# More buffers for two small operands, and a later back transpose, in the gated-DeltaNet part of a hybrid encoder layer

## The chip, the cores and the metric

The kernel runs on one core of one Trainium2 chip. The metric is the device time of one execution in microseconds (us); the number given for a kernel is the median of several runs. The engines of the core are named as in the profile: PE (TensorE, matrix products and transposes; PEld is its weight load), DVE (VectorE), ACT (ScalarE), POOL (GpSimd) and SP (SyncE, which here only issues DMAs; its queue is written SPq).

## The reference: what is computed

One encoder layer over x of 2048 rows by 1024 columns. One combined projection of the normalised x is split into the inputs of three mixing branches and a gate z; the three outputs are joined, multiplied by silu(z), projected back and added to x:

```python
h = rms_norm(x, norm_pre_w[l])
proj = h @ w_in[l]
aq, ak, av, bqkv, ba, bb, mq, z = jnp.split(proj, pts, axis=-1)
# A: softmax attention, 8 query heads, 2 key heads, rotary positions
y_a = axial_gqa_attention(aq, ak, av)
# B: gated DeltaNet, 4 heads of width 128, both directions, chunks of 64
bqkv = centred_short_conv(bqkv, conv_w[l])          # 5 taps, then silu
bq, bk, bv = (t.reshape(b, s, B_HEADS, HEAD_DIM) for t in jnp.split(bqkv, 3, axis=-1))
y_b = bidir_gated_deltanet(bq, bk, bv, ba, bb, a_log[l], dt_bias[l])
#   g = -exp(a_log) * softplus(ba + dt_bias);  beta = sigmoid(bb)
#   q and k are divided by their norms; g is summed up inside a chunk;
#   per chunk: k k^T and q k^T times exp(g_i - g_j), a triangular solve,
#   then a scan over the chunks
# M: cross-attention of 4 heads into 256 memory rows
y_m = memory_cross_attention(mq, mk, mv)
mix = jnp.concatenate([y_a, y_b, y_m], axis=-1) * jax.nn.silu(z)
x = x + rms_norm(mix @ w_out[l], norm_post_w[l])
```

Everything that the change touches belongs to branch B.

## The kernel before, in words

The program is one function. Its loops emit instructions in the written order; a planner then simulates a timeline with its own durations and from it fixes, once and for all, the order of the instructions of each engine. Stretches where `pin(...)` is on keep their written order on the engines named. Each engine works through its list in order; where engines depend on each other they wait on semaphores. All operations go through a small wrapper, so the profile shows line L51 for nearly everything, and L77 for the DMAs that POOL issues; the names of the tiles tell them apart. A tile's `bufs` is the number of rooms that its successive uses take in turn.

The stages, with the times at which they stand in the profiled execution:

- 0 to 328 us: loads, normalisation of x, and the projections of branches A and M.
- **Stage s2** (L584 to L694), 328 to about 631 us: the q, k and v of branch B. There are 48 slots: 12 groups of 128 channels (`ch` 0 to 3 are q, 4 to 7 are k, 8 to 11 are v) by 4 blocks of 512 rows (`b`). Each slot goes through four steps at different lags. `b_proj` (lag 0) makes 24 matmuls into the PSUM tile `b` and copies it to `xb` on ACT. `b_conv` (lag 2) is the five-tap convolution, five DVE instructions into `y`, a tanh on ACT (`th`) and one DVE instruction into `sv`. `b_turn` (lag 5) transposes `sv` on PE, into `bs` for q and into `bt` for k and v. For q, ACT squares and sums it. For v, ACT copies it to `kt`, which goes to DRAM (`bx`). For k, ACT squares it, DVE reduces it (`kss`) and runs a short chain of 128x4 instructions for the inverse root (`rs_x`, `rs_u`, `kr`), DVE multiplies into `kt`, and `kt` goes to `bx`. `b_back` (lag 7, k only) transposes `kt` back on PE into `bu`; ACT copies that to `ku`, which goes to `bx` too. The same slots also carry small side work: `wor` (loads and squares of w_out, an ACT instruction behind a DMA each) and `v` (a split of branch A's values).
- `fill(48)` (L816) emits the first steps of the z projection; after it PE is pinned to the written order (L817). `fill(n)` always means n more matmuls, with what belongs to them, of the z and mq projections. Per 24 matmuls of z: `zt` (tanh on ACT), `zg` (DVE) and a `gate` DMA on POOL's queue; every second group of channels also has new weights `wraw` and `wparts`, made by POOL, ACT and DVE.
- **The gate part of stage s3** (L820 to L906): 72 fill matmuls; then, in pool `s3g`, softplus and sigmoid of the per-row gates: a chain of 128x128 DVE instructions over `xa`, `ax`, `u`, `s_`, `s` and `acc` with exponentials on ACT, which ends in `gg` and `beta`. `psg` is the product of `gg` with a triangle on PE, 40 fill matmuls follow, then transposes `gr` into the table `grow`, which stage s3a reads.
- **Stage s3a** (L909 to L932), about 650 to 755 us: 32 turns (two head pairs by 16 chunks of 128 rows, pool `s3r`). A turn loads `kq` (the chunk's back-transposed k, and q) from `bx`, multiplies it on PE (`pg`), makes the decay exponents on PE (`pe`), exponentials on ACT (`dd`), five DVE products into `nit`, a DMA of `nit` to `NI`, and 10 fill matmuls.
- Then, on DVE, the triangular inverse of all chunks of a head pair (L935 to L961): `ni` is loaded from `NI` by 16 small DMAs, and pairs of `tm`/`rr` instructions follow. The `ni` loads of head pair 0 stand in SP's queue among the turns of head pair 1.
- From about 850 us: the scan of branch B, the attention of A and M, and the output projection.

The lines that the change touches stand in `b_turn` (L635), in the slot loop (L687 and L692) and in the s3a loop (L914):

```python
kt = p.tile([128, 4, 128], F32, tag="kt", name=f"kt{ch}_{b}", bufs=2)          # L635
for n in range(len(slots) + 7):                                                # L687
    for lag, f in ((0, b_proj), (2, b_conv), (5, b_turn), (7, b_back)):        # L692
kq = p.tile([128, 2, 2, 128], F32, tag="kq", name=f"kq{nm}", bufs=3)           # L914
```

Of the kernel before, what the change touches and what calls it, by code (L numbers as in the profile page):

```python
# [11 lines left out]
F32 = mybir.dt.float32  # L12
# [25 lines left out]
def hybrid_layer(ctx: ExitStack, tc: tile.TileContext, t: dict, out, dbg=None):  # L38
# [238 lines left out]
    def load_group(*args, **kw):  # L277
        _, loaded = begin_group(*args, **kw)
        return loaded
# [177 lines left out]
    with tc.tile_pool(name="s1", bufs=1) as p:  # L457
# [49 lines left out]
        for which in range(2):  # L507
# [20 lines left out]
            for g in range(1 if which == 0 else 4):  # L528
                wg, (qcs,) = nxt
                for b in range(4):  # L530
# [4 lines left out]
                    nm = f"{which}_{g}_{b}"  # L535
# [48 lines left out]
    with tc.tile_pool(name="s2", bufs=1) as p:  # L584
        wg, bcs, xbs, svs, kts_ = {0: nxt[0]}, {0: nxt[1]}, {}, {}, {}

        def b_proj(ch, b):
            g, u = ch // 2, ch % 2
            if u == 1 and b == 0:
                if g < 5:  # L590
                    wg[g + 1], bcs[g + 1] = load_group([(1536 + 256 * (g + 1), 256)])
                else:
                    _, wg[6] = z_load(4)
            if b == 0:
                xb = xbs[ch] = p.tile([128, S + 4], F32, tag="xb", name=f"xb{ch}", bufs=2)
                V.memset(xb[:, 0:2], 0.0)
                V.memset(xb[:, S + 2:S + 4], 0.0)
            ps = mm_ps(f"b{ch}_{b}")
            n = 0
            for kc in range(KC):  # L600
                hi, lo = wg[g][kc // 4]
                sl = slice(u * 128, u * 128 + 128)
                for wt, ht in ((hi, 0), (hi, 1), (lo, 0)):
                    T.matmul(ps, wt[:, kc % 4, sl], hT[b][ht][:, kc, :], start=(n == 0), stop=(n == 3 * KC - 1))
                    n += 1
            A.activation(xbs[ch][:, 2 + 512 * b:2 + 512 * (b + 1)], ps, AF.Copy, scale=bcs[g][0])

        def b_conv(ch, b):
            xb, o = xbs[ch], 512 * b
            y = p.tile([128, 512], F32, tag="y", name=f"y{ch}_{b}", bufs=2)  # L610
            V.tensor_scalar(y, xb[:, o:o + 512], convw[:, ch, 0:1], None, op0=ALU.mult)
            for k in range(1, 5):
                V.scalar_tensor_tensor(y, xb[:, o + k:o + k + 512], convw[:, ch, k:k + 1], y, op0=ALU.mult, op1=ALU.add)
            th = p.tile([128, 512], F32, tag="th", name=f"th{ch}_{b}", bufs=2)
            A.activation(th, y, AF.Tanh)
            sv = svs[ch, b] = p.tile([128, 4, 128], F32, tag="sv", name=f"sv{ch}_{b}", bufs=2)
            V.scalar_tensor_tensor(sv.rearrange("p a b -> p (a b)"), th, 1.0, y, op0=ALU.add, op1=ALU.mult)

        def b_turn(ch, b):
            kind, hd = ch // 4, ch % 4  # L620
            hp, hh = hd // 2, hd % 2
            sv = svs.pop((ch, b))
            if kind == 0:
                dma(bx(hp, b, 1, hh), sv)
                pt = tp_ps(f"bs{ch}_{b}", (128, 4, 128))
                sq = p.tile([128, 4, 128], F32, tag="sq", name=f"sq{ch}_{b}")
                for j in range(4):
                    T.transpose(pt[:, j, :], sv[:, j, :], ident)
                for j in range(4):
                    A.activation(sq[:, j, :], pt[:, j, :], AF.Square, accum_out=ssq[:, hd, 4 * b + j:4 * b + j + 1])  # L630
                return
            pt = tp_ps(f"bt{ch}_{b}", (128, 4, 128))
            for j in range(4):
                T.transpose(pt[:, j, :], sv[:, j, :], ident)
            kt = p.tile([128, 4, 128], F32, tag="kt", name=f"kt{ch}_{b}", bufs=2)  # L635
            if kind == 2:
                A.copy(kt, pt)
                dma(bx(hp, b, 3, hh), kt)
                return
            sq = p.tile([128, 4, 128], F32, tag="sq", name=f"sq{ch}_{b}")  # L640
            A.activation(sq, pt, AF.Square)
            ks = p.tile([128, 4], F32, tag="kss", name=f"kss{ch}_{b}", bufs=2)
            V.tensor_reduce(ks, sq, axis=AX.X, op=ALU.add)
            kr = p.tile([128, 4], F32, tag="kr", name=f"kr{ch}_{b}", bufs=2)
            rsqrt(p, kr, ks, [128, 4], 1.0, EPS)
            V.tensor_tensor(kt, pt, kr.unsqueeze(2).to_broadcast([128, 4, 128]), op=ALU.mult)
            dma(bx(hp, b, 2, hh), kt)
            kts_[ch, b] = kt

        def b_back(ch, b):  # L650
            if (ch, b) not in kts_:
                return
            kt = kts_.pop((ch, b))
            hp, hh = (ch % 4) // 2, ch % 2
            pt = tp_ps(f"bu{ch}_{b}", (128, 4, 128))
            for j in range(4):
                T.transpose(pt[:, j, :], kt[:, j, :], ident)
            ku = p.tile([128, 4, 128], F32, tag="ku", name=f"ku{ch}_{b}")
            A.copy(ku, pt)
            dma(bx(hp, b, 0, hh), ku)  # L660

        def wo_sums(kc):

            raw = p.tile([128, D], F32, tag="wor", name=f"wor{kc}")
            dma(raw, t["w_out"][0, kc * 128:(kc + 1) * 128, :])
            A.activation(raw, raw, AF.Square, accum_out=wosq[:, kc // 2, kc % 2:kc % 2 + 1])

        v32s, v16s = {}, {}

        def v_split(tb, k):  # L670

            if k == 0:
                v32s[tb] = p.tile([128, 256], F32, tag="v32", name=f"v32_{tb}")
                dma(v32s[tb], v_d[tb])
                v16s[tb] = p.tile([128, 2, 256], F16, tag="v16", name=f"v16_{tb}")
                return
            pin(A, V)
            if k == 1:
                A.activation(v16s[tb][:, 0], v32s[tb], AF.Copy, scale=vs)
            else:  # L680
                v = v16s.pop(tb)
                V.scalar_tensor_tensor(v[:, 1], v32s.pop(tb), vs, v[:, 0], op0=ALU.mult, op1=ALU.subtract)
                dma(v16_d[:, :, tb, :], v)
            pin()

        slots = [(ch, b) for ch in range(12) for b in range(4)]
        for n in range(len(slots) + 7):  # L687
            if n < 3 * TB:
                v_split(n // 3, n % 3)
                if n % 3 == 1:  # L690
                    wo_sums(n // 3)
            for lag, f in ((0, b_proj), (2, b_conv), (5, b_turn), (7, b_back)):  # L692
                if 0 <= n - lag < len(slots):
                    f(*slots[n - lag])  # L694
    first_z = wg[6]
# [213 lines left out]
    with tc.tile_pool(name="s3a", bufs=1) as sv0:  # L909
        p = rows  # L910
        for hp in range(2):
            for c in range(TB):
                nm = f"{hp}_{c}"
                kq = p.tile([128, 2, 2, 128], F32, tag="kq", name=f"kq{nm}", bufs=3)  # L914
                dma(kq, bx_d[hp, c, :, 0:2])
                pg = tp_ps(f"pg{nm}", (128, 2, 2, 128))
                for h in range(2):
                    T.matmul(pg[:, :, h, :], kq[:, 0, h, :], kq[:, :, h, :], start=True, stop=True)
                pe = tp_ps(f"pe{nm}", (128, 2, 2, 128))
                T.matmul(pe, pick[:, c:c + 1].to_broadcast([96, 128]), grow[:, :, 2 * hp:2 * hp + 2, :], start=True, stop=False)  # L920
                T.matmul(pe, identb, maskb, start=False, stop=True)
                dd = p.tile([128, 2, 2, 128], F32, tag="dd", name=f"dd{nm}", bufs=2)
                for d in range(2):
                    for h in range(2):
                        A.activation(dd[:, d, h, :], pe[:, d, h, :], AF.Exp, bias=ngc[:, d, 2 * hp + h, c:c + 1])
                ni = p.tile([128, 2, 2, 2, 128], F32, tag="nit", name=f"nit{nm}", bufs=2)
                V.tensor_tensor(ni[:, :, 1], dd, pg[:, 1].unsqueeze(1).to_broadcast([128, 2, 2, 128]), op=ALU.mult)
                for d in range(2):
                    for h in range(2):
                        V.scalar_tensor_tensor(ni[:, d, 0, h, :], pg[:, 0, h, :], beta[:, d, 2 * hp + h, c:c + 1], dd[:, d, h, :], op0=ALU.mult, op1=ALU.mult)  # L930
                dma(NI_d[hp, :, c].rearrange("d p n h i -> p d (n h i)"), ni.rearrange("p d n h i -> p d (n h i)"))
                fill(FILL[1])  # L932
        pr_pool.close()
        sv1 = pr_pool.enter_context(tc.tile_pool(name="s3c", bufs=1, side="right"))
        for hp in range(2):  # L935
            p = (sv0, sv1)[hp]
# [226 lines left out]
    p = p5.enter_context(tc.tile_pool(name="at", bufs=1))  # L1163
    kt, vt, PT = at["k"], at["v"], at["PT"]
# [267 lines left out]
    for i in range(len(blocks) + LAG + 1):  # L1432
# [27 lines left out]
        for tb in range(2):  # L1460
            n = i - len(blocks) - 2 * tb - LAG + 4
# [43 lines left out]
    with ExitStack() as es:  # L1505
        p = es.enter_context(tc.tile_pool(name="op", bufs=1))
# [101 lines left out]
```

## Time and profile before

| what | us |
|---|---|
| median of 3 runs | 2408.82 (2407.42 to 2410.19) |
| the profiled execution | 2418.02 |
| its span, first to last instruction | 2416.0 |
| PE busy | 2316.7 (96%) |
| DVE busy | 1637.6 (68%) |
| ACT busy | 1298.9 (54%) |
| POOL busy | 703.2 (29%) |
| mean granted clock of PE | 0.989 |

Rows of a timeline give the start in us, the duration, the engine, line, operation, "out<-in" with its shapes, the number of instructions in the row (xN) and, in brackets, the idle time of the engine just before it with the instruction or DMA whose end released it. A row of windows gives a stretch of the span, its length, and the busy time and number of instructions of PE, PEld, DVE, ACT and POOL; then the clock granted to PE (1.00 is full), the share of the DMA engines that was busy and the rate in GB/s. A row of groups gives the instructions of one kind, their count, their busy time in us and the mean in ns, and the idle time ahead of them.

### The profile page before, as it was taken

Reading aid. Unit: us, or ns where it says so; the run is one execution under the profiler, and the core shown is the slowest. Engines: PE = TensorE matmul, PEld = TensorE weight load, DVE = VectorE, ACT = ScalarE, POOL = GpSimd, SP = SyncE. Lnnn points to the kernel's source line nnn. Section 1 sums busy time; section 2 is a strip of 40 time slices with the busy share of each in tenths; the row PEclk is TensorE's granted clock in tenths of the full one; section 3 lists DMA queues with packets and bytes.
Section 4 is the critical chain, followed back from the end, with each engine's and each line's share of the span. In section 5 each row is a group of like instructions: output and inputs, shape, how many; then the busy total and the mean of one; then the engine's idle time right before and its main releaser. Section 6 shows DMA issues by size and latency. Waiting matters only on the chain. (4 is left out here: it accounts for less than half of the span.)

```text
span 2416.0 us, 42155 instructions
## 1 busy us (share of the span) xinstructions
PE 2316.7 (96%) x15838; PEld 1466.6 (61%) x15846; DVE 1637.6 (68%) x3304; ACT 1298.9 (54%) x2508; POOL 703.2 (29%) x432
## 2 busy tenths in 40 slices
PE   6999999999999899999999999999999999899998
PEld 6888864455554347667664566666666666544443
DVE  6687658999758745555553778777888877355553
ACT  5634436544443145555543888888888788111110
POOL 0155431112211221121020554444444445122120
PEclk9999999999999999999999999999999999999999
DMA  6457656334487466677865999999999999775551
GB/s 232 144 137 162 123 118 188 101 111 126 146 254 214 106 201 212 205 221 219 249 201 192 232 248 242 246 240 244 239 250 241 246 240 231 202 248 187 178 183 53
DMA packets 949500, 471.58 MB, mean 195 GB/s; under 512 B 723184, under 2 KB 898864, under 8 KB 949040
## 3 DMA queue, kind: packets, MB, share of 16 engines
q1 hardware_dynamic: 936848, 425.89, 69.6%
q0 software_dynamic: 12448, 43.00, 5.3%
q8 instruction: 125, 2.05, 0.3%
q14 instruction: 79, 0.65, 0.1%
HBM read 207.60 MB, written 108.10 MB: 131 GB/s over the span
## 5 line engine op out<-in xcount | busy, mean ns | idle before, releaser
L51 PEld LDWEIGHTS <-wparts 128*128 128x128 f16 x3072 | 294.9, 99 | 324.2 <-issue 18.1
L51 POOL TENSOR_TENSOR hla<-Pa,hla 128x1281 f16<-128x1281 f32 x128 | 335.8, 2624 | 343.1 <-DVE hla L51 320.2
L51 DVE TENSOR_REDUCE mxa<-sa 128x1 f32<-128x1024 f32 x256 | 313.1, 1223 | 132.3 <-PE sa L51 132.2
L51 PE MATMUL sa<-K,qa 128*128 128x512 f16 x1536 | 373.8, 379 | 21.2 <-ACT Pa L51 10.0
L51 PE MATMUL z<-hT,wparts 128*128 128x512 f16 x1536 | 378.4, 384 | 4.1 <-POOL wparts L51 2.9
L51 PE MATMUL pva<-PT,V 128*128 128x256 f16 x3072 | 376.4, 273 | 0.0
L51 ACT ACTIVATE Pa<-sa,mxa,misc 128x1024 f32<-128x1024 f32 x256 | 305.9, 1199 | 97.8 <-POOL hla L51 81.0
L51 PEld LDWEIGHTS <-V 128*128 128x128 f16 x3072 | 300.6, 98 | 84.9
L51 PE MATMUL o<-wo,mhl 128*128 128x512 f16 x1416 | 309.5, 382 | 6.3 <-ACT mhl L51 3.8
L51 PE MATMUL b<-hT,wparts 128*128 128x512 f16 x1152 | 258.1, 381 | 0.0
L51 PEld LDWEIGHTS <-mhl 128*128 128x128 f16 x1464 | 143.7, 98 | 181.9 <-DVE mhl L51 4.2
L51 PEld LDWEIGHTS <-qa 128*128 128x128 f16 x1536 | 150.1, 98 | 157.0 <-issue 27.0
L51 ACT CAST hla<-Pa 128x2048 f16<-128x2048 f32 x128 | 243.0, 1899 | 4.2
L51 PEld LDWEIGHTS <-hT 128*128 128x128 f16 x2304 | 224.8, 98 | 30.4 <-DVE we L51 1.7
L51 PE MATMUL q<-wparts,hT 128*128 128x256 f16 x1920 | 210.3, 273 | 1.4 <-DVE we L51 1.4
L77 POOL DMA_DIRECT2D gate<-zg x64 | 35.4, 554 | 423.7 <-DVE zg L51 288.1
L51 POOL TENSOR_SCALAR wraw<-wraw,wsc 128x1024 f32<-128x1024 f32 x21 | 69.1, 3292 | 288.4 <-DVE wy L51 197.5
L51 ACT CAST mhl<-mr 128x2048 f16<-128x2048 f32 (+1 forms) x16 | 29.1, 1818 | 221.7 <-PE o L51 172.8
L51 DVE SCALAR_TENSOR_TENSOR y<-xb,convw,y 128x512 f32<-128x512 f32 x192 | 145.8, 771 | 2.0
L51 POOL TENSOR_TENSOR mg<-mg 128x1536 f32<-128x1536 f32 (+1 forms) x16 | 59.4, 3712 | 234.1 <-DMA mg<-r 171.2
L51 DVE SCALAR_TENSOR_TENSOR hla<-Pa,hla 128x768 f16<-128x768 f32 x128 | 121.6, 950 | 0.0
L51 DVE TENSOR_TENSOR mhl<-mr,mhl 128x2048 f16<-128x2048 f32 (+1 forms) x16 | 45.2, 2824 | 89.3 <-ACT mhl L51 89.3
(354 smaller groups left out, 3165.4 us busy)
## 6 DMA issues: line engine op xcount, KB each, us to landing
xx<-bx SPq DMA_DIRECT2D x64, 512.0 KB, 6.0
wraw<-in_w_in POOLq DMA_DIRECT2D x42, 512.0 KB, 5.3
wor<-in_w_out SPq DMA_DIRECT2D x32, 512.0 KB, 4.3
gate<-zg POOLq DMA_DIRECT2D x64, 256.0 KB, 4.0
NI<-nit SPq DMA_DIRECT2D x32, 512.0 KB, 3.0
mr<-mix SPq DMA_DIRECT2D x13, 1024.0 KB, 6.1
mg<-r SPq DMA_DIRECT2D x13, 768.0 KB
x<-in_x SPq DMA_DIRECT2D x16, 512.0 KB, 6.3
```

The costliest lines, as they stand in the source:

```text
L51: ins = f(*args, **kw)
L77: nc.gpsimd.dma_start(to, of)
```

## The change

Three constants are changed; no operation is added or removed.

```diff
@@ -632,7 +632,7 @@
             pt = tp_ps(f"bt{ch}_{b}", (128, 4, 128))
             for j in range(4):
                 T.transpose(pt[:, j, :], sv[:, j, :], ident)
-            kt = p.tile([128, 4, 128], F32, tag="kt", name=f"kt{ch}_{b}", bufs=2)
+            kt = p.tile([128, 4, 128], F32, tag="kt", name=f"kt{ch}_{b}", bufs=3)
             if kind == 2:
                 A.copy(kt, pt)
                 dma(bx(hp, b, 3, hh), kt)
@@ -684,12 +684,12 @@
             pin()
 
         slots = [(ch, b) for ch in range(12) for b in range(4)]
-        for n in range(len(slots) + 7):
+        for n in range(len(slots) + 8):
             if n < 3 * TB:
                 v_split(n // 3, n % 3)
                 if n % 3 == 1:
                     wo_sums(n // 3)
-            for lag, f in ((0, b_proj), (2, b_conv), (5, b_turn), (7, b_back)):
+            for lag, f in ((0, b_proj), (2, b_conv), (5, b_turn), (8, b_back)):
                 if 0 <= n - lag < len(slots):
                     f(*slots[n - lag])
     first_z = wg[6]
@@ -911,7 +911,7 @@
         for hp in range(2):
             for c in range(TB):
                 nm = f"{hp}_{c}"
-                kq = p.tile([128, 2, 2, 128], F32, tag="kq", name=f"kq{nm}", bufs=3)
+                kq = p.tile([128, 2, 2, 128], F32, tag="kq", name=f"kq{nm}", bufs=5)
                 dma(kq, bx_d[hp, c, :, 0:2])
                 pg = tp_ps(f"pg{nm}", (128, 2, 2, 128))
                 for h in range(2):
```

A `kt` room is 2,048 bytes per partition, a `kq` room also. The pool s2 grows up from the left of the memory; the pools s3r (with `kq`) and s3g (with the softplus tiles, behind s3r) grow down from the right. In the built program before, s2 ends at byte 188,032 of a partition and s3g begins at 192,160. In the changed one s2 ends at 190,080 (one `kt` room more) and s3g begins at 188,064 (two `kq` rooms lower). So there 2,016 bytes belong to both: `xa`, `ax`, `u` and `s_` of the softplus lie over bytes of s2, and the planner lets the first of them wait until s2 is released, which the last `kt` and its DMA do.

The order of the instructions changes on every engine between the q slots of s2 and the gate part of s3, and on SP also in s3a; before and after that it is the same. Three places are shown.

The first is DVE's list at the end of s2, where the last two `sv` of the v channels (s2's last work on DVE) are followed by what comes next. Before:

```order
L51 SCALAR_TENSOR_TENSOR sv_2_7028<-th_2_7026,y_2_7020 128x512
L51 SCALAR_TENSOR_TENSOR sv_3_7046<-th_3_7044,y_3_7038 128x512
L51 TENSOR_TENSOR gg<-acc,nal 128x64 x2
L51 TENSOR_TENSOR beta<-u,s__7294 128x128
L51 TENSOR_SCALAR rs_x<-ssq 128x64
L51 TENSOR_SCALAR qs<-rs_x 128x64
L51 SCALAR_TENSOR_TENSOR zg_0_7115<-zt_0_7113,z_0_7088 128x512
```

In the changed kernel the place begins so (`qs`, `rs_x` and `rs_u` are the inverse norms of q, which both kernels compute here):

```order
L51 SCALAR_TENSOR_TENSOR sv_3_7046<-th_3_7044,y_3_7038 128x512
L51 TENSOR_TENSOR xa<-ab,dtb 128x64 x2
L51 TENSOR_SCALAR rs_x<-ssq 128x64
L51 TENSOR_SCALAR ax<-xa 128x128
L51 TENSOR_SCALAR qs<-rs_x 128x64
L51 TENSOR_TENSOR ax<-ax,xa 128x128
L51 SCALAR_TENSOR_TENSOR zg_0_7115<-zt_0_7113,z_0_7088 128x512
L51 SCALAR_TENSOR_TENSOR rs_u<-qs 128x64
L51 SCALAR_TENSOR_TENSOR zg_1_7159<-zt_1_7157,z_1_7132 128x512
```

and 42 rows further on it reads:

```order
L51 TENSOR_SCALAR acc<-acc 128x128
L51 SCALAR_TENSOR_TENSOR zg_0_7265<-zt_0_7263,z_0_7238 128x512
L51 TENSOR_TENSOR acc<-acc,s__7294 128x128
L51 SCALAR_TENSOR_TENSOR acc<-xa,acc 128x128
L51 TENSOR_TENSOR gg<-acc,nal 128x64 x2
L51 COPY xa<-ab 128x64 x2
L51 TENSOR_SCALAR ax<-xa 128x128
```

So the whole softplus, which stood among the q slots (`xa` between the convolutions some 550 rows earlier), now stands behind the last `sv`, and `gg` behind it, where `gg` was the first instruction; the five `zg`, the `qs` chain and one `wparts` stand ahead of `gg` instead of behind it. `psg` has the same place on PE in both.

The second place is ACT's list among the q slots. Before:

```order
L51 ACTIVATE xb_4325<-b_1_4366,wc_3744 128x512
L51 ACTIVATE wor_4464,wosq<-wor_4464 128x1024
L51 ACTIVATE sq_0_4404,ssq<-bs_0_4403 128x128 x4
L51 ACTIVATE wor_4617,wosq<-wor_4617 128x1024
L51 ACTIVATE xb_4325<-b_2_4416,wc_3744 128x512
L51 ACTIVATE th_2_4360<-y_2_4354 128x512
```

Now:

```order
L51 ACTIVATE xb_4325<-b_1_4366,wc_3744 128x512
L51 ACTIVATE wor_4464,wosq<-wor_4464 128x1024
L51 ACTIVATE sq_0_4404,ssq<-bs_0_4403 128x128 x4
L51 ACTIVATE th_2_4360<-y_2_4354 128x512
L51 ACTIVATE th_3_4398<-y_3_4392 128x512
L51 ACTIVATE xb_4325<-b_2_4416,wc_3744 128x512
```

The tanh of this slot has moved ahead of a `wor`, which needs a load of w_out.

The third place is SP's queue where s3a goes from head pair 0 to head pair 1 (`kq_3` to `kq_8` and `nit_0` on are of pair 1, `nit_14` and `nit_15` of pair 0, `ni` are the loads for the triangular inverse of pair 0). Before:

```order
L51 DMA NI<-nit_15_7971 128x2x512
L51 DMA kq_3_8090<-bx 128x512
L51 DMA ni_8529<-NI 16x32x32
L51 DMA NI<-nit_0_8007 128x2x512
L51 DMA kq_4_8125<-bx 128x512
L51 DMA ni_8529<-NI 16x32x32 x5
L51 DMA NI<-nit_1_8037 128x2x512
L51 DMA kq_5_8156<-bx 128x512
L51 DMA ni_8529<-NI 16x32x32 x6
```

Now:

```order
L51 DMA NI<-nit_15_7971 128x2x512
L51 DMA kq_5_8156<-bx 128x512
L51 DMA ni_8529<-NI 16x32x32
L51 DMA NI<-nit_0_8007 128x2x512
L51 DMA kq_6_8186<-bx 128x512
L51 DMA ni_8529<-NI 16x32x32 x5
L51 DMA NI<-nit_1_8037 128x2x512
L51 DMA kq_7_8222<-bx 128x512
L51 DMA ni_8529<-NI 16x32x32 x6
```

Every `kq` of s3a stands two turns earlier against the `NI` and `ni` DMAs, whose order among themselves is unchanged. On PE, each `bu` moves behind the next `bt` (the first from the middle of a `b` group to its end, 21 rows later), and the `bs` of the q slots move some 12 to 16 rows earlier.

## The prediction, made before the changed kernel was run

> **What bounds the kernel now.** The first view is the page's busy time, the second the windows, to see who sets the pace in the stretches that the change touches.
>
> ```profile
> PE 2316.7 (96%) x15838; PEld 1466.6 (61%) x15846; DVE 1637.6 (68%) x3304; ACT 1298.9 (54%) x2508; POOL 703.2 (29%) x432
> ...
> 328.00:450.00 122.00, 119.34 (x587) 58.09 (x585) 98.62 (x209) 71.17 (x219) 18.61 (x14) 1.00 0.55 153
> 450.00:470.00 20.00, 16.84 (x84) 8.26 (x82) 19.23 (x39) 10.55 (x25) 6.65 (x4) 1.00 0.21 67
> 470.00:580.00 110.00, 108.99 (x561) 57.34 (x562) 107.00 (x319) 46.15 (x78) 14.14 (x8) 0.98 0.40 116
> 580.00:612.00 32.00, 32.00 (x169) 16.94 (x168) 31.77 (x57) 17.50 (x30) 7.79 (x4) 1.00 0.47 138
> 612.00:650.00 38.00, 38.00 (x195) 19.56 (x194) 27.18 (x64) 14.07 (x26) 9.84 (x10) 1.00 0.33 104
> ```
>
> PE is busy for 96% of the span, so the end moves when PE waits, or stops waiting. In the q slots (328 to 450) PE sets the pace: it idles 2.66 us of 122, DVE 23.4. From 450 to 612 DVE is nearly full, idle for 0.77, 3.00 and 0.23 us, 4.0 in all: the k slots are bound by DVE. PE does not suffer, since it has other work. From 612 to 650 PE has no gap. The PE timeline, the third view, shows its two waits in this stretch, and what a wait leaves behind:
>
> ```profile
> 373.84 0.66 PE L51 MATMUL bs<-ident,sv 128*128 128x128 f32 x4 [2.40 <-DVE sv L51]
> ...
> 471.01 0.86 PE L51 MATMUL bu<-ident,kt 128*128 128x128 f32 x4 [4.17 <-DVE kr L51]
> 471.66 3.82 PE L51 MATMUL b<-hT,wparts 128*128 128x512 f16 x10
> ...
> 743.03 2.32 PE L51 MATMUL mq<-hT,wparts 128*128 128x512 f16 x10
> ```
>
> The second is the wait at which the later `b_back` aims: the first `bu`, 4.17 us. Ten projection matmuls took 3.82 us behind it and 2.32 elsewhere, 1.50 more. So the wait is worth 4.17 + 1.50 = 5.7 us of PE.
>
> The Trainium skill, page "TensorE: Matmul & The Clock Gate", Part 1, puts such slow matmuls down to a gate that halves the clock after an idle window of some 3.4 us and opens it after as long a busy one. By it, as an estimate, a wait costs 1.7 us more; the row says 1.50, and the row is used.
>
> **The change, part by part.**
>
> *Where the softplus goes.* The order shows that the extra rooms make the softplus tiles lie over s2, so its chain now waits until s2 is released. What stands at that release, on DVE, and when `psg` was due on PE:
>
> ```profile
> 624.83 0.69 DVE L51 SCALAR_TENSOR_TENSOR sv<-th,y 128x512 f32<-128x512 f32 x1 [0.15 <-ACT th L51]
> 631.45 0.36 DVE L51 TENSOR_TENSOR gg<-acc,nal 128x64 f32<-128x64 f32 x2 [5.93 <-DMA bx<-kt]
> 631.72 0.28 DVE L51 TENSOR_TENSOR beta<-u,s__7294 128x128 f32<-128x128 f32 x1
> ...
> 632.86 0.22 DVE L51 SCALAR_TENSOR_TENSOR rs_u<-qs 128x64 f32<-128x64 f32 x1
> ...
> 637.00 0.69 DVE L51 SCALAR_TENSOR_TENSOR zg<-zt,z 128x512 f32<-128x512 f32 x1 [1.57 <-DMA gate<-zg]
> ...
> 641.25 0.68 DVE L51 SCALAR_TENSOR_TENSOR zg<-zt,z 128x512 f32<-128x512 f32 x1
> ```
>
> ```profile
> 639.67 0.55 PE L51 MATMUL psg<-gg,tri 128*128 128x64 f32 x4
> 640.34 8.80 PE L51 MATMUL z<-hT,wparts 128*128 128x512 f16 x40
> ```
>
> Before, `gg` was finished at 631.8 and PE came to `psg` only at 639.67: 7.9 us of slack. In the new order everything that DVE did from 631.45 to the end of the `zg` at 641.25 (641.93) stands ahead of `gg`, and with it the softplus. Its instructions, as they ran among the q slots:
>
> ```profile
> 351.72 0.42 DVE L51 TENSOR_TENSOR xa<-ab,dtb 128x64 f32<-128x64 f32 x2
> ...
> 353.84 0.22 DVE L51 TENSOR_SCALAR ax<-xa 128x128 f32<-128x128 f32 x1
> ...
> 359.19 0.94 DVE L51 RECIPROCAL s__7294<-s__7294 128x128 f32<-128x128 f32 x1
> ...
> 364.11 0.28 DVE L51 TENSOR_TENSOR s<-s__7294 128x128 f32<-128x128 f32 x1
> ```
>
> ```profile
> L51 DVE TENSOR_TENSOR acc<-acc,s 128x128 f32<-128x128 f32 x8 | 2.3, 282 | 0.0
> ...
> L51 DVE TENSOR_SCALAR acc<-acc 128x128 f32<-128x128 f32 x8 | 1.8, 220 | 0.1
> ```
>
> The `xa` pair 0.42, the reciprocal 0.94, the sixteen steps of `acc` 4.1, five more two-input instructions (`ax`, `s_`, `s`, the last two of `acc`) at 0.28 are 1.40, four more scalar ones (`ax`, `s_`, the first `acc`, `nal`) at 0.22 are 0.88: 7.74 us. Two things come off: the 1.57 us for which a `zg` waited on a `gate` DMA, since there is now other work ahead of it, and `beta` (0.28), which goes behind `gg`. So `gg` is done at 641.93 + 7.74 - 1.57 - 0.28 = 647.8 us if s2 is released when it was.
>
> *What POOL does to it.* The chain now runs beside the two POOL instructions of the next weights:
>
> ```profile
> 638.55 2.85 POOL L51 TENSOR_SCALAR wraw<-wraw,wsc 128x1024 f32<-128x1024 f32 x1
> ...
> 642.78 2.13 POOL L51 TENSOR_TENSOR wparts<-wraw,wparts 128x1024 f16<-128x1024 f32 x1
> ```
>
> ```profile
> 638.69 1.07 DVE L51 SCALAR_TENSOR_TENSOR qs<-qs 128x64 f32<-128x64 f32 x1
> ...
> 642.86 2.15 DVE L51 TENSOR_SCALAR ngam<-gam 128x128 f32<-128x128 f32 x1 [0.94 <-ACT gam L51]
> ```
>
> Against 0.22 us for their like, `qs` lost 0.85 beside the first, and `ngam` 1.93 beside the second. The 0.85 is in the 641.93 already. The second fell behind the DVE work of the tail; in the new order it falls among the steps of `acc`. The cost is at least 0 and at most what is left of both, 2.85 - 0.85 + 2.13 = 4.1; I take the row's 1.9. That gives 649.7.
>
> The Trainium skill, page "SBUF — State Buffer", section "Who interferes with whom", speaks against the change here: the second ports of DVE and GpSimd are one pair under an exclusive lock, and a DVE instruction with two SBUF inputs or in a two-port mode waits out a whole GpSimd instruction. `ngam` agrees, with 2.15 us beside 2.13; the first POOL instruction cost only one such wait.
>
> *When s2 is released.* The first wait above (2.40) hung on a tanh that stood behind a squared `wor`:
>
> ```profile
> 370.82 1.06 ACT L51 ACTIVATE wor<-wor 128x1024 f32<-128x1024 f32 x1 [4.47 <-DMA wor<-in_w_out]
> ...
> 373.09 0.69 DVE L51 SCALAR_TENSOR_TENSOR sv<-th,y 128x512 f32<-128x512 f32 x1 [1.89 <-ACT th L51]
> ```
>
> In the new order the tanh stands ahead of that `wor`, so I count the 2.40 us as gained: PE sets the pace there, so the k and v slots start and end 2.4 us earlier. Their DVE work is the same. The softplus's leaving the q slots gives DVE nothing more, since it has 23.4 us to spare there. Bounds: nothing gained (0), or also all of the 4.0 us of idle DVE (6.4). So `gg` comes at 649.7 - 2.4 = 647.3.
>
> *The wait removed, and the new one.* The first `bu` now stands behind `bt` and 10 matmuls later (2.3 us or more of the 4.17); with a third `kt` room the DVE side need not hold back. But the 5.7 and the 2.4 us that PE saves before 640 only bring it to `psg` sooner, where it now waits for `gg`. So these are worth nothing while `gg` is late; if its cover were gone, 8.1. Behind `psg` in PE's order stands everything else. It starts at 647.3 instead of 639.67, +7.7; the wait is longer than the 4.17 above, so the slow matmuls behind it (+1.5) come with it: +9.2 at the `gr` transposes. `gp`, which those need, is ten small DVE instructions behind `psg`, about 2.6 us at 0.22 to 0.28 each; the 40 fill matmuls (8.80) hide it, as they hide `beta`'s chain.
>
> *The five rooms of `kq`.* They act from 714 to 742 us:
>
> ```profile
> PE pg L51 <- DMA kq<-bx: 5.9, 4, 2.4
> ...
> DVE nit L51 <- DMA NI<-nit: 10.6, 4, 3.5
> ```
>
> ```profile
> 715.58 1.03 PE L51 MATMUL pg<-kq 128*128 128x256 f32 x4
> ...
> 741.73 1.03 PE L51 MATMUL pg<-kq 128*128 128x256 f32 x4
> ...
> 745.19 1.03 PE L51 MATMUL pg<-kq 128*128 128x256 f32 x4
> ```
>
> ```profile
> 729.56 0.69 DVE L51 TENSOR_TENSOR nit<-dd,pg 128x512 f32<-128x512 f32 x1 [3.51 <-DMA NI<-nit]
> ...
> 733.30 2.12 DVE L51 COPY rr<-ni 64x2048 f32<-64x2048 f32 x1 [2.01 <-DMA NI<-nit]
> ...
> 736.71 0.69 DVE L51 TENSOR_TENSOR nit<-dd,pg 128x512 f32<-128x512 f32 x1
> ```
>
> A normal turn takes 3.46 us (741.73 to 745.19). The five turns from 715.58 to 741.73 took 26.15, 8.85 more, with 5.9 us of waits for `kq`. Two turns earlier in SP's queue, each `kq` is there in time. But next late is `nit`: its two rooms come free with the `NI` DMAs, which stand in SP's queue behind the `ni` loads as before, and that cost DVE 10.6 us. `pg` and `pe` have four PSUM rooms together, so PE can be two turns ahead of `nit` and no more. The turn of 736.51 could then start behind the `nit` of 729.56 and one turn's work, about 734: a gain of some 2.4 us for PE, none for DVE, whose `nit` at 736.71 follows that copy and the one back, which nothing makes earlier. And what PE gains it may lose again where DVE's triangular inverse holds it:
>
> ```profile
> 796.96 2.14 DVE L51 COPY rr<-ni 64x2048 f32<-64x2048 f32 x1 [9.50 <-DMA ni<-NI]
> ...
> 805.09 7.24 PE L51 MATMUL mq<-hT,wparts 128*128 128x512 f16 x25 [4.42 <-DVE mqo L51]
> ```
>
> Bounds 0 and 2.4; I take 1.0. Earlier in SP's queue, two `kq` more wait behind a `ku` of the k slots and can hold `kt` and `ku` DMAs for a few us; ACT, which copies `ku`, is idle more than half of that stretch and hides it.
>
> *Sum.* +7.7 (late `psg`) + 1.5 (slow matmuls) - 1.0 (`kq`) = +8.2 us: the profiled execution goes from 2418.02 to 2426.2. That execution stands 9.2 above the median of 2408.82; its difference is carried over, which gives a median of 2417.0.
>
> **The rivals.**
>
> B, *the `kq` gain sticks*. All of 8.85 us is saved because the `NI` DMAs, too, come earlier once PE is not held. Then 9.2 - 8.85 = +0.3: 2409.1, not slower. For it speaks that every one of PE's waits there names `kq`; against it the 10.6 us of DVE on `NI`, and that SP issues the `ni` loads at its own pace. It decides once more than half of 8.85 reaches the mq matmuls at 805.
>
> C, *POOL blocks it all*: 4.1 instead of 1.9, so +10.4: 2419.2. For it speaks `ngam`, against it the single loss beside the first POOL instruction. It is the rule cited above.
>
> D, *s2 ends earlier still*: with the third `kt` room DVE's 4.0 us of idle time go as well, and POOL costs nothing. `gg` at 647.8 - 6.4 = 641.4, so +1.7 + 1.5 - 1.0 = +2.2: 2411.0. Against it: those gaps are spread over 160 us, and the short `kr` chains make them, which stay.
>
> E, *B and D together*: 2.2 + 1.0 - 8.85 = -5.6: 2403.2, faster.
>
> That the later `bu` still waits for its `kt` is possible, but changes nothing as long as `psg` waits.
>
> **How the numbers follow.** My forecast has 0.56, C 0.17, B 0.12, D 0.10, E 0.05. A measurement of this kernel can tell about 0.2%, 4.8 us, from no change. Faster: E and little else, 0.06. Within 0.2%: B, D, and the lower edge of the forecast less what of B and D lies outside, 0.21. Slower: the rest, 0.73. The forecast's own bounds go from +0.8 (`gg` at 641.4, `kq` 2.4) to +13.8 (s2 not earlier, POOL 4.1, `kq` 0: 651.9 at `psg`). The range from 2410.0 to 2422.0 leaves out about 0.18: E, the lower half of B, and the upper end of C.
>
> **What would show it.** In the changed kernel's profile: no wait of 4 us at the first `bu` and none of 2.4 at the third `bs`; the chain `xa` to `gg` behind the last `sv`; PE idle for about 10 us or more ahead of `psg`, released by DVE `acc` or `gg`, at 646 to 650 us; slow z matmuls behind it; a DVE step of about 2 us beside POOL's second instruction; the waits of `pg` for `kq` gone, with waits on `nit` in their place. I am wrong if `psg` starts before 643, or if the stretch from `psg` to the mq matmuls at 805 shrinks by more than 4 us.

## The result, and the profile after

The changed kernel took 2421.69 us (median of 6 runs, 2415.93 to 2427.62) against 2407.66 us (2406.07 to 2410.19) of the kernel before on the same chip: a ratio of 1.0059, with a 95% interval of 1.0044 to 1.0075, or about 14 us more. The forecast was 2417.0, slower, with a range from 2410.0 to 2422.0.

The two profiled executions do not show these 14 us in their spans (2417.4 after, 2416.0 before). The profiled execution before stands 10 us over its median, and one stage probably accounts for most of that: from the last mq matmul to the first attention matmul, where the change moves no instruction, it took 476.1 us, the changed kernel 467.3, and the ten profiled kernels below anything from 460.5 to 475.2. So the traces are compared up to that stage, and the times in runs taken side by side.

The places where PE waits in the stretch of the change, from PE's timeline of the changed kernel:

```profile
438.65 0.63 PE L51 MATMUL bs<-ident,sv 128*128 128x128 f32 x4 [3.12 <-ACT th L51]
...
474.83 0.63 PE L51 MATMUL bu<-ident,kt 128*128 128x128 f32 x4 [1.82 <-DVE kr L51]
...
482.20 0.63 PE L51 MATMUL bt<-ident,sv 128*128 128x128 f32 x4 [1.56 <-DVE kt L51]
...
576.71 0.66 PE L51 MATMUL bt<-ident,sv 128*128 128x128 f32 x4 [2.22 <-ACT ku L51]
...
654.28 1.08 PE L51 MATMUL psg<-gg,tri 128*128 128x64 f32 x4 [7.33 <-issue]
655.15 0.74 PE L51 MATMUL psg<-gg,ones 128*128 128x128 f32 x2
```

The wait at the third `bs` (2.40 us before) is gone, and the one at the first `bu` has shrunk from 4.17 to 1.82. But new ones stand at a later `bs` and at two `bt`. `psg` starts at 654.28 instead of 639.67, behind 7.33 us of idle PE. The profile names no releaser for that wait ("issue"); DVE's timeline does:

```profile
629.86 0.69 DVE L51 SCALAR_TENSOR_TENSOR sv<-th,y 128x512 f32<-128x512 f32 x1 [0.70 <-ACT th L51]
637.15 0.43 DVE L51 TENSOR_TENSOR xa<-ab,dtb 128x64 f32<-128x64 f32 x2 [6.61 <-DMA bx<-kt]
...
642.50 0.69 DVE L51 SCALAR_TENSOR_TENSOR zg<-zt,z 128x512 f32<-128x512 f32 x1 [0.99 <-DMA gate<-zg]
...
645.54 0.78 DVE L51 TENSOR_TENSOR acc<-acc,s 128x128 f32<-128x128 f32 x1
...
649.12 2.24 DVE L51 TENSOR_TENSOR acc<-acc,s 128x128 f32<-128x128 f32 x1
...
653.95 0.36 DVE L51 TENSOR_TENSOR gg<-acc,nal 128x64 f32<-128x64 f32 x2
```

`xa`, the head of the softplus, waits for the last `kt` DMA, s2's release; `gg` ends at 654.31, 17.2 us behind it, when `psg` starts. Two steps of `acc` were longer than their 0.28 us, each beside one of POOL's instructions, which POOL's timeline has here:

```profile
645.07 2.85 POOL L51 TENSOR_SCALAR wraw<-wraw,wsc 128x1024 f32<-128x1024 f32 x1 [1.05 <-DVE wsc L51]
...
649.10 2.11 POOL L51 TENSOR_TENSOR wparts<-wraw,wparts 128x1024 f16<-128x1024 f32 x1 [0.62 <-ACT wparts L51]
```

The tile views give the first and last start of each tile's matmuls (mean durations in between). For `b`, `gr` and `mq`, first of the kernel before, then of the changed one:

```profile
L51 PE MATMUL b<-hT,wparts x1152: 376/379/634, 327.9 to 610.9; 128*128 128x512 f16 x192
...
L51 PE MATMUL gr<-ident,gp x8: 272/272/273, 649.0 to 649.7; 128*96 128x128 f32 x8
...
L51 PE MATMUL mq<-hT,wparts x384: 376/379/635, 732.6 to 837.7; 128*128 128x512 f16 x192
```

```profile
L51 PE MATMUL b<-hT,wparts x1152: 376/379/631, 330.7 to 618.0; 128*128 128x512 f16 x192
...
L51 PE MATMUL gr<-ident,gp x8: 272/272/273, 666.1 to 666.8; 128*96 128x128 f32 x8
...
L51 PE MATMUL mq<-hT,wparts x384: 377/379/634, 748.5 to 851.3; 128*128 128x512 f16 x192
```

The first `b` matmul, ahead of everything that the change touches, stands 2.8 us later in the second trace, and anywhere from 325.4 to 330.7 in the traces below. Measured from it, the `gr` transposes stand at 321.1 before and 335.4 after (+14.3), the last mq matmul at 509.8 and 520.6 (+10.8). Three profiled kernels stand close to each other ahead of `psg`: the kernel before, the one with five `kq` rooms alone and the one before with the softplus series three times. In all three the softplus runs among the q slots, `b_back` has lag 7 and `wor` one room; their orders are not quite the same. They spread by 3 us at `gr` and by 5 at the last mq matmul (the table at the end of the experiments), so such differences are good to some 2 or 3 us.

### The profile page after: what moved, and what is told of

Same layout as the page of the kernel before. It is cut to its first block, busy times and chain, and to the rows that moved or that the text cites. A ratio compares the mean times of both kernels' runs of the same rounds, so it can differ in the third digit from the quotient of the medians.

```text
span 2417.4 us, 42154 instructions
## 1 busy us (share of the span) xinstructions
PE 2313.0 (96%) x15846; PEld 1464.0 (61%) x15846; DVE 1636.4 (68%) x3304; ACT 1298.0 (54%) x2508; POOL 702.3 (29%) x432
## 5 line engine op out<-in xcount | busy, mean ns | idle before, releaser
L51 PEld LDWEIGHTS <-wparts 128*128 128x128 f16 x3072 | 294.3, 98 | 319.0 <-issue 13.5
```

Source lines behind the costliest of these rows:

```text
L51: ins = f(*args, **kw)
```

## The experiments

Three theories were set against each other. Theory 1: the loss comes from the 2,016 bytes in which the softplus tiles lie over s2, and from nothing else in the change. Theory 2: it comes from the third `kt` room and the later `bu`. Theory 3: it comes from the two `kq` loads more that wait in SP's queue among the k slots. Each kernel was timed beside the kernel before on the same chip; a ratio is to that one, with its 95% interval.

**The overlap alone.** The edit gives `ku` six kilobytes that nothing uses, and leaves the three constants as they were:

```diff
-            ku = p.tile([128, 4, 128], F32, tag="ku", name=f"ku{ch}_{b}")
+            ku = p.tile([128, 16, 128], F32, tag="ku", name=f"ku{ch}_{b}")[:, 0:4]
```

> The kernel before with one edit: the tile ku is made 8,192 bytes per partition instead of 2,048 (its first quarter is used), so that s2 ends at byte 194,176 and lies over the same 2,016 bytes of the softplus tiles as in the changed kernel. kt keeps two rooms, kq three, the lag stays 7. Theory 1 (the loss comes from the overlap alone, and the five kq rooms gave back some 3.5 us of it): psg at 650 to 656 us instead of 639.7, and a time of about 2425 (2419 to 2429), slower even than the changed kernel. Theory 2 (the loss comes from the later bu and the third kt room) and theory 3 (it comes from the two kq more that wait in SP's queue among the k slots): 2408, within 3 us of the kernel before.

Measured: 1.0060 (1.0043 to 1.0077), the ratio of the changed kernel. In PE's timeline the same two waits stand as in the changed kernel, at a `bs` and at `psg`:

```profile
435.75 1.09 PE L51 MATMUL bs<-ident,sv 128*128 128x128 f32 x4 [3.95 <-ACT th L51]
...
650.98 1.09 PE L51 MATMUL psg<-gg,tri 128*128 128x64 f32 x4 [10.24 <-issue]
```

With no operation and none of the three constants changed, a bigger tile does it all: the softplus stands behind s2 and the order of ACT in the q slots changes, as in the changed kernel, and the time is lost. Theory 1 holds; theories 2 and 3 are not needed for the loss. The part of its expectation that the time would lie above the changed kernel's (by the missing `kq` gain) did not come true.

**The third `kt` room and lag 8 alone.**

```diff
-            kt = p.tile([128, 4, 128], F32, tag="kt", name=f"kt{ch}_{b}", bufs=2)
+            kt = p.tile([128, 4, 128], F32, tag="kt", name=f"kt{ch}_{b}", bufs=3)
...
-        for n in range(len(slots) + 7):
+        for n in range(len(slots) + 8):
...
-            for lag, f in ((0, b_proj), (2, b_conv), (5, b_turn), (7, b_back)):
+            for lag, f in ((0, b_proj), (2, b_conv), (5, b_turn), (8, b_back)):
```

> The kernel before with the third kt room and b_back at lag 8 only; kq keeps three rooms, so nothing overlaps and the softplus stays among the q slots. Theory 1: the wait of 4.2 us at the first bu goes, but PE has then to wait for the zg of the first z unit, which hangs on s2's release as before; a gain of 0 to 2 us, 2406 (2403 to 2409). Theory 2: slower by 5 us or more (2413 to 2422), with s2 released some 5 us later. Theory 3: as theory 1.

Measured: 1.0016 (1.0001 to 1.0030), 0 to 7 us slower: theory 1's gain of 0 to 2 us did not come. Theory 2's 5 us are inside the interval, so the time does not exclude it, but `psg`, at 313.1 us behind the first `b` matmul, is 10 us short of the changed kernel's 323.6. The wait at the first `bu` is gone, but one came in its place. PE's timeline, and ACT's at the same place:

```profile
570.10 0.66 PE L51 MATMUL bt<-ident,sv 128*128 128x128 f32 x4 [2.63 <-ACT ku L51]
```

```profile
569.06 0.51 ACT L51 ACTIVATE v<-v,scales 128x256 f16<-128x256 f32 x1 [3.90 <-DMA v<-v]
569.48 0.57 ACT L51 COPY ku<-bu 128x512 f32<-128x512 f32 x1
```

The `bt` needs a PSUM room that the `ku` copy frees, and the copy stands on ACT behind an instruction of the side work that waits 3.9 us for its load. (With lag 8, the built programs with two and with three `kt` rooms have the same order on PE, DVE and ACT. The third room alone was not timed.)

**Five `kq` rooms alone.**

```diff
-                kq = p.tile([128, 2, 2, 128], F32, tag="kq", name=f"kq{nm}", bufs=3)
+                kq = p.tile([128, 2, 2, 128], F32, tag="kq", name=f"kq{nm}", bufs=5)
```

> The kernel before with five kq rooms only; s2 ends 32 bytes below s3g, so nothing overlaps. Theory 1: the waits of pg for kq (5.9 us in four places) go, waits on nit come in their place, and about 3.5 us are left: 2404 (2401 to 2408). Theory 3: slower by 3 us or more, with s2 released later. My forecast's own figure for this part was a gain of 1.0 (0 to 2.4).

Measured: 1.0001 (0.9990 to 1.0013): nothing, which refutes theory 1's 3.5 us. Theory 3's 3 us are at the edge of the interval, but s2, which was to be released later, is released at 300.8 us behind the first `b` matmul, where the kernel before has 303.6; so theory 3 fails too. PE's waits from 632 to 860 us, grouped (engine, tile and line, what it waited for: us in total, times, longest):

```profile
PE mq L51 <- DVE mqo L51: 5.5, 1, 5.5
PE pe L51 <- DVE nit L51: 3.6, 2, 2.4
PE z L51 <- POOL wparts L51: 2.1, 1, 2.1
```

The 5.9 us of waits of `pg` for `kq` are gone. In their place `pe` waits 3.6 us for `nit`, and the wait for `mqo` behind the triangular inverse grew from 4.42 to 5.5. From `gr` to the last mq matmul it takes 188.1 us instead of 188.7.

**All three edits, made not to overlap by a smaller s3g.** `gp`, `gb` and `gr` were taken from another pool, so that s3g is smaller:

```diff
-        gp = p.tile([128, 8, 3, 32], F32, tag="gp", name="gp")
-        gb = p.tile([128, 8, 3, TB], BF16, tag="gb", name="gb")
-        gr = p.tile([128, 8, TB], F32, tag="gr", name="gr")
+        gp = bp.tile([128, 8, 3, 32], F32, tag="gp", name="gp")
+        gb = bp.tile([128, 8, 3, TB], BF16, tag="gb", name="gb")
+        gr = bp.tile([128, 8, TB], F32, tag="gr", name="gr")
```

> All three edits of the change, and gp, gb and gr (4,352 bytes) taken from the pool bp instead of s3g, so that s3g begins at byte 192,416 and nothing overlaps. Theory 1: the sum of the two parts, a gain of about 5 us: 2403 (2399 to 2407). Theories 2 and 3: slower by 10 us or more, as the changed kernel is (2417 to 2423).

Measured: 1.0048 (1.0034 to 1.0062), slower by 11.6 us, against what theory 1 expected. The profile shows that this loss is not made where the overlap acts. `psg` is back at 642.6 us, and the last mq matmul, 506.4 us behind the first `b` matmul, is not later than in the kernel before (509.8). PE's timeline has a new wait far behind:

```profile
878.40 2.72 PE L51 MATMUL z<-hT,wparts 128*128 128x512 f16 x6 [6.22 <-DVE zg L51]
```

With bp 4,352 bytes larger, the order of DVE and ACT differs from before's as far as the stage behind s3a, not only up to it. From the last mq matmul to the first attention matmul it takes 473.1 us, against 465.9 and 466.5 in the profiles of the two preceding kernels, taken on the same chip. So the loss is put down to the probe itself; this is argued, since that stage varies as much from one profile to another.

**All three edits with four `kq` rooms instead of five.** That ends s2 32 bytes below s3g.

```diff
-                kq = p.tile([128, 2, 2, 128], F32, tag="kq", name=f"kq{nm}", bufs=3)
+                kq = p.tile([128, 2, 2, 128], F32, tag="kq", name=f"kq{nm}", bufs=4)
```

> The third kt room, lag 8 and four kq rooms instead of five: s2 ends at byte 190,080 and s3g begins at 190,112, so nothing overlaps, and the order after s2 is that of before but for kq. It takes the place of the probe that moved gp, whose order changed after 834 us as well and lost time there. Theory 1 (the overlap is the loss): as the third kt room and lag 8 alone, 0 to 4 us above the kernel before, psg at 310 to 314 us behind the first b matmul. Theory 3 (kq waits in SP's queue among the k slots): 5 us or more above the kernel with three kq rooms.

Measured: 1.0004 (0.9992 to 1.0016). One `kq` room less than in the changed kernel, and the 14 us are gone. PE's waits from 325 to 632 us are for the most part of the kind that the two edits alone have (`bt` 2.7 us for `ku` and 1.6 for `kt`; a `bu` waits 1.5 as well), and `psg` stands 312.9 us behind the first `b` matmul; the two edits alone have 313.1. This is theory 1's number.

**The softplus lengthened.** The `acc` series is computed three times, once in the changed kernel and once in the kernel before; the result is the same.

```diff
-        V.tensor_scalar(acc, s2, 2.0 / 19, 2.0 / 17, op0=ALU.mult, op1=ALU.add)
-        for k in (15, 13, 11, 9, 7, 5, 3, 1):
-            V.tensor_tensor(acc, acc, s2, op=ALU.mult)
-            V.tensor_scalar(acc, acc, 2.0 / k, None, op0=ALU.add)
+        for _ in range(3):
+            V.tensor_scalar(acc, s2, 2.0 / 19, 2.0 / 17, op0=ALU.mult, op1=ALU.add)
+            for k in (15, 13, 11, 9, 7, 5, 3, 1):
+                V.tensor_tensor(acc, acc, s2, op=ALU.mult)
+                V.tensor_scalar(acc, acc, 2.0 / k, None, op0=ALU.add)
```

> The changed kernel with the acc series of the softplus computed three times instead of once (the first two results are thrown away), 34 small DVE instructions more, at 0.59 us a pair 10.0 us. If the softplus is on the path ahead of psg: psg 10 us later than in the changed kernel, and the whole some 9 to 10 us slower than it, so about 23 us above the kernel before (ratio 1.009 to 1.011). If psg waits for something else (s2, POOL, the z work): within 3 us of the changed kernel.

> The kernel before with the acc series computed three times, the same 34 instructions more. There the softplus stands among the q slots, where DVE idles some 23 us of 122: within 3 us of the kernel before (0 to +3). If DVE's time in the q slots sets the end of s2 after all: +7 to +10.

Measured: the changed kernel goes to 1.0108 (1.0090 to 1.0127), 0.0049 or 11.8 us more than with one series. The kernel before stays at 0.9997 (0.9986 to 1.0008). In the first, DVE's timeline has the two ends of the chain 27.2 us apart instead of 16.8, and PE waits 10.4 us longer:

```profile
637.64 0.43 DVE L51 TENSOR_TENSOR xa<-ab,dtb 128x64 f32<-128x64 f32 x2 [6.60 <-DMA bx<-kt]
...
664.83 0.36 DVE L51 TENSOR_TENSOR gg<-acc,nal 128x64 f32<-128x64 f32 x2
```

```profile
665.15 1.08 PE L51 MATMUL psg<-gg,tri 128*128 128x64 f32 x4 [17.72 <-issue]
```

(`psg` stands 13.1 us later behind the first `b` matmul, 2.6 of it from a later release in this trace.) So behind s2 the DVE instructions of the softplus are paid in full; among the q slots, 34 more cost nothing.

**Why s2 is released later.** In the changed kernel `xa` starts 306.45 us behind the first `b` matmul, in the kernel before `gg` at 303.55, where an earlier release was forecast. ACT's waits from 325 to 450 us, before and then after:

```profile
ACT wor L51 <- DMA wor<-in_w_out: 18.7, 11, 4.5
```

```profile
ACT wor L51 <- DMA wor<-in_w_out: 27.6, 16, 2.7
```

ACT waits 16 times instead of 11 for a load of w_out, whose one room must first be squared; behind these stand the `xb` copies and tanhs that feed DVE. The overlap alone, with lag 7, has the same: 16 waits, 29.4 us, and a release at 306.0. The next two kernels give `wor` a second room, one on top of the change and one on the kernel before:

```diff
-            raw = p.tile([128, D], F32, tag="wor", name=f"wor{kc}")
+            raw = p.tile([128, D], F32, tag="wor", name=f"wor{kc}", bufs=2)
```

> The changed kernel with two rooms for wor (the loads of w_out beside the q slots), so that a load need not wait for the square before it. s2 overlaps s3g as before, by 4,096 bytes more. If the later release of s2 (some 4 us, measured from the first b matmul) comes from the tanh and xb instructions that stand on ACT behind squares waiting for their loads: ACT's waits for wor (19 us in 388 to 446) go down to a few us, the waits of bs on th go, s2 is released 3 to 5 us earlier, and the time is some 3 to 5 us below the changed kernel (ratio 1.004 to 1.005). If not: within 2 us of the changed kernel.

Measured: the ratio is 1.0043 (1.0025 to 1.0061). ACT's waits for `wor` fall to 8.6 us, and `xa` starts at 625.74 us, 298.6 behind the first `b` matmul, 7.8 earlier than in the changed kernel:

```profile
625.74 0.43 DVE L51 TENSOR_TENSOR xa<-ab,dtb 128x64 f32<-128x64 f32 x2 [6.60 <-DMA bx<-kt]
...
642.88 0.36 DVE L51 TENSOR_TENSOR gg<-acc,nal 128x64 f32<-128x64 f32 x2
```

The chain from `xa` to `gg` is about as long as without this edit (17.1 us from start to start, 16.8 there), so `psg` comes 7.5 us earlier. That the loads of w_out hold up s2's end is shown by this. In the time, 0.0016 or 4 us is the size expected, but the two intervals overlap; it is not settled there.

> The kernel before with two rooms for wor and nothing else; s2 then ends at byte 192,128, 32 below s3g, so nothing overlaps. If the q slots are held up by ACT instructions that stand behind squares waiting for their loads in this kernel as well (ACT waits 18 us for wor there): sv of the last q slot 5 to 7 us earlier, s2 released 3 to 5 us earlier, psg (which no softplus holds) 3 to 6 us earlier, and a time some 3 to 5 us below the kernel before (ratio 0.998 to 0.9985). If DVE alone sets the end of s2: within 2 us of it.

Measured: 0.9970 (0.9959 to 0.9982), 7 us faster than the kernel before, and so faster than both. In its profile s2 is released 295.8 us behind the first `b` matmul and `psg` starts at 304.0 (before: 303.55 and 311.8). DVE's and PE's rows:

```profile
623.76 0.36 DVE L51 TENSOR_TENSOR gg<-acc,nal 128x64 f32<-128x64 f32 x2 [5.12 <-DMA bx<-kt]
```

```profile
PE bs L51 <- DVE sv L51: 0.9, 1, 0.9
```

The second is all that is left of PE's waits from 325 to 632 us. The wait at the first `bu`, at which lag 8 aimed, is gone with lag 7 and two `kt` rooms.

The loads of w_out hold up both kernels, then, and the second room brings the release forward by about as much in the one (7.8 us) as in the other (7.8, or 5.9 against the mean of the three profiles named under the result). With two rooms in both, the changed kernel is still released 2.8 us later (298.6 against 295.8). So these runs do not show that the longer waits for w_out are the whole difference between the two kernels. They leave some 3 us, about the uncertainty of such a comparison; the nearest candidate is a wait of a `bt` for `ku` (3.0 us in the profile of the changed kernel with two `wor` rooms), of the kind that came with lag 8; it was not separated.

**The side work's other load.** Lag 8 and the third `kt` room, with a second room for the loads of `v`:

```diff
-                v32s[tb] = p.tile([128, 256], F32, tag="v32", name=f"v32_{tb}")
+                v32s[tb] = p.tile([128, 256], F32, tag="v32", name=f"v32_{tb}", bufs=2)
```

> The third kt room and lag 8 with three kq rooms, and two rooms for v32 (the loads of the values that ACT splits beside the slots). In the profile of the two edits alone a bt waited 2.6 us for a ku copy that stood on ACT behind a v instruction waiting 3.9 us for its load. If that is what costs the two edits their 0 to 4 us: the wait of bt on ku is gone and psg comes 1.5 to 3 us earlier, behind the first b matmul, than the 313.1 of the two edits alone. If the wait has another root (the single ku room): it stays. The planner orders ACT and DVE differently here too, so the time itself, expected within 3 us of the kernel before, tells less than the waits.

Measured: 0.9993 (0.9981 to 1.0005). The waits of `bt` for `ku` are down to 0.3 us, `psg` stands at 309.7 instead of 313.1. This agrees with the rows above, by which the wait that lag 8 brought in came from the load that ACT waited for. As the order of ACT and DVE changed in many rows, and other waits came (1.8 us at the first `bu`, 1.6 at a `bt`), this run alone does not prove it.

The places in the profiles, in us behind the first `b` matmul (the release is the start of DVE's first instruction behind the last `kt` DMA):

| kernel | ratio | release | `psg` | `gr` | last mq |
|---|---|---|---|---|---|
| before | 1 | 303.6 | 311.8 | 321.1 | 509.8 |
| five `kq` | 1.0001 | 300.8 | 308.6 | 317.9 | 506.0 |
| before, series three times | 0.9997 | 300.7 | 308.9 | 318.2 | 505.1 |
| third `kt`, lag 8 | 1.0016 | 302.9 | 313.1 | 322.4 | 510.4 |
| third `kt`, lag 8, four `kq` | 1.0004 | 302.8 | 312.9 | 322.2 | 508.4 |
| third `kt`, lag 8, two `v32` | 0.9993 | 300.3 | 309.7 | 319.0 | 507.2 |
| all three edits, smaller s3g | 1.0048 | 305.0 | 315.0 | 324.3 | 506.4 |
| changed | 1.0059 | 306.5 | 323.6 | 335.4 | 520.6 |
| overlap alone | 1.0060 | 306.0 | 324.6 | 337.1 | 523.3 |
| changed, series three times | 1.0108 | 309.1 | 336.7 | 348.1 | 536.5 |
| changed, two `wor` | 1.0043 | 298.6 | 316.1 | 327.3 | 511.0 |
| before, two `wor` | 0.9970 | 295.8 | 304.0 | 313.3 | 500.4 |

## Why the prediction was right, and where it was not

The direction and the cause held. The range held by luck: 2421.69 is 0.3 us under its upper edge, and the kernel before came out at 2407.66 in the same runs, not at the 2408.82 on which the forecast stood; the measured rise of 14 us on top of that would be about 2423. That the softplus behind s2 decides, and that the saved waits are swallowed by the new one, was the forecast's reason; the overlap alone and the lengthened series show it. The size, +8.2 against +14, was off, for one term above all.

**When s2 is released: forecast 2.4 us earlier, measured later.** From the first `b` matmul the release moved by +2.9 in the two traces, and by +4.8 against the mean of the three profiles named under the result (301.7). This step failed. I saw the tanh move ahead of one `wor` and counted the wait behind it as gained. I didn't follow the same list to its end, where the later squares stand so that ACT waits 27.6 us for them instead of 18.7 and a new wait of 3.12 us comes at a later `bs`. That this order goes with a later release is shown by the overlap alone (306.0); how much of the delay is due to the longer waits for w_out stays open, as said above. The bounds given (0 to 6.4 us earlier) left out a loss, which nothing in the profile excluded.

**The softplus chain: forecast 18.3 us from release to `gg` (649.7 against 631.45), measured 17.2.** The total was right to 1 us, but by two errors that cancel in part. The `zg` still waited 0.99 us for its `gate` DMA, where I took that wait as gone. POOL cost 0.5 and 1.96 (0.78 and 2.24 less 0.28 each) where 0.85 and 1.9 were taken; rival C's 4.1 did not come. What is left for the instructions themselves is 13.7 us, where 15.5 were summed: I added up durations, and in the trace an instruction often starts before the one ahead of it has ended (`zg` at 642.50 for 0.69, the next at 643.10).

**`psg` late: forecast +7.7, measured +11.8** from the first `b` matmul (+14.6 on the clock of the trace). PE's wait there was to be 10 us or more, ending at 646 to 650; it was 7.33, ending at 654.28. The slow matmuls behind it: forecast +1.5; from `psg` to `gr` it takes 11.8 us instead of 9.3, so +2.5.

**The saved waits: forecast worth nothing while `gg` is late.** Right as a term: the third `kt` room and lag 8 change nothing in the sum of the changed kernel, which is as slow as the overlap alone. But the saving behind it did not take place. PE was to reach `psg` 8.1 us sooner; it was done with everything ahead of `psg` at 646.95 us, 316.3 behind the first `b` matmul, where the kernel before started `psg` at 311.8. Its waits from 325 to 632 us had grown from 6.9 to 9.6 us. That cost nothing here, since `gg` came later still. Nor does the cover taken away give the 8.1 us that I priced: with no overlap the two edits give 0, or a loss of up to 0.3%; a wait at `bt` stands in the place of the one at `bu`.

**Five `kq` rooms: forecast -1.0, between 0 and 2.4; measured 0** (-2.4 to +3.1 us by the interval of the ratio). The waits moved to `nit` and `mqo`, as said. This also rules out rivals B and E, which had all of 8.85 us.

**Rival D**, an earlier release still, went the wrong way, as the first step did.

The sum with the measured terms: +11.8 at `psg` and +2.5 behind it are +14.3 at `gr`. From `gr` to the last mq matmul 3.5 us are made up (185.2 us instead of 188.7, where the three profiles lie between 186.9 and 188.7); in the overlap alone, without the five `kq` rooms, it is 2.5 (186.2). So what is made up there is for the most part not theirs, and what makes it up was not tried. Against the mean of the three profiles (309.8 at `psg`, 319.1 at `gr`, 507.0 at the last mq), the same places are +13.8, +16.3 and +13.6, and the last agrees with the 14 us of the runs.

## What to carry to other kernels

Before a room is added, look where its bytes come from: here two rooms and one pushed two pools into each other by 2,016 bytes, which let a whole chain of small instructions wait for the release of the other pool, at a price of 14 us, while the rooms themselves brought nothing. When an order changes, follow the whole list of the engine that feeds the bound one, not the one place where a wait was seen; the instructions that wait for a load are the ones to count. And a wait at one instruction (the first `bu`) may only be where an earlier delay comes out: the second room for `wor`, which changes the order in the q slots ahead of it, removed it, with 7 us of gain.

## What was not expected of the hardware

A DVE instruction on two 128x128 operands that met POOL's `wparts` instruction took 2.24 us instead of 0.28, beside 2.11 us of POOL's; the one that met POOL's `wraw` instruction took 0.78, though that one lasted 2.85. The forecast had the two sizes (1.93 and 0.85 over the usual) from a scalar instruction and a small one; that larger ones with two operands lose about as much was open. It was the same in two more profiles (0.79 and 2.24 or 2.25); in the overlap alone, an `acc` step with two operands took 2.71 beside 2.13 of POOL's. The slow matmuls behind `psg` cost 2.5 us for 7.33 us of idle PE, where 1.50 us were lost behind 4.17. The loss does not grow with the wait: from `psg` to `gr`, the three other profiles with a wait there lost 1.9 us behind 7.67, 3.2 behind 10.24 and 2.1 behind 17.72.
